# Contrast adjustment, streamed: from twelve tiles of 32 KB rows in six buffers to six tiles of 64 KB rows in three

## The chip, the cores and the metric

The kernel runs on one core of one Trainium2 chip. The core's engines appear in the profile under short names: PE is TensorE (its weight loads are PEld), DVE is VectorE, ACT is ScalarE, POOL is GpSimd and SP is SyncE. Data moves between the chip's main memory (DRAM) and the core's on-chip buffer (the SBUF, 128 partitions) by DMA, and sixteen DMA engines do the moving. A DMA is put into a queue by the engine that issues it: here SP issues all loads (the profile calls that queue q1) and ACT issues all stores (q10). The metric is the device time of one execution in microseconds (us), as the median of several runs. The hardware profiler recorded one execution; its lines are quoted with that execution's own times, counted from the start of its span.

## The reference

The input is sixteen images of three channels of 512 x 512 pixels in 32-bit floats, 50.33 MB. Every channel of every image is pulled away from its own mean and clipped:

```python
def reference(x, factor):                      # factor = 1.5
    mean = np.mean(x, axis=(2, 3), keepdims=True)
    return np.clip(mean + factor * (x - mean), 0, 1).astype(np.float32)
```

This is `clip(factor * x + (1 - factor) * mean)`. A channel's output cannot start before all of that channel has been read. Each byte has to be read once and written once: 100.66 MB in all.

## The kernel before

The input is seen as one flat run of numbers. A tile is 128 rows of ROW = 8192 numbers (32 KB), one row to a partition, 4.19 MB in all; a row is contiguous in DRAM. A channel has 262,144 pixels, so 32 neighbouring partitions hold one channel and a tile holds four channels. There are twelve tiles, t = 0 to 11. One SBUF tensor named ring holds six of them (BUFS = 6); tile t lies in place t modulo 6, and all work on it is done in place. With 32 KB per partition and tile, the ring takes 192 KB of each partition.

Four steps are done on a tile:

- `load(t)` (L82, on SP's queue) fetches the tile. The first two tiles come as one DMA each, tiles 2 and 3 as one DMA of 8.39 MB, tiles 4 and 5 as another, and the rest as one DMA each. From tile 6 on, a load may only begin when the store of the tile six before it has landed; SP waits for that before it issues the load.
- `add(t)` takes the sums. ACT copies the tile onto itself and accumulates a sum per partition (L96). For tile 0 alone the work is shared: DVE sums the first 4352 columns (L91) and ACT the other 3840. Then PE multiplies the sums by a matrix that adds up the 32 partitions of a channel and scales by (1 - factor) / 262144 (L100), and the result, called bias, stands in PSUM, one number per partition.
- `clip(t)` is two DVE instructions on the tile: times factor plus bias (L104), then the clip to 0 and 1 (L112).
- `store(t)` (L85, on ACT's queue) writes the tile out.

The order is written out by hand; each engine does its instructions in the order in which the program gives them, and waits where a result that it needs is not there. Tile 0 is clipped and stored in three pieces of 1024, 2048 and 5120 columns (FIRST gives the cuts), that is in rows of 4, 8 and 20 KB. After that comes a loop over the tiles: clip, then the sums of the next tile, then the store and a load:

```python
for t in range(1, n_tiles):
    clip(t)
    if t in (1, 3): store(t)
    if t + 1 < n_tiles: add(t + 1)
    if t not in (1, 3): store(t)
    if t + BUFS - 1 < n_tiles: load(t + BUFS - 1)
```

A store therefore stands on ACT mostly behind the sums of the next tile, and waits for the clip.

Of the kernel before, what the change touches and what calls it, by code (L numbers as in the profile page):

```python
# [1 line left out]

# [4 lines left out]


P = 128  # L10
ROW = 8192
BUFS = 6
FIRST = (1024, 3072)


@with_exitstack
def kernel(
    ctx: ExitStack,
    tc: tile.TileContext,
    x: bass.AP,  # L20
    factor: float,
    out: bass.AP,
):

    nc = tc.nc
    f32 = mybir.dt.float32
    Alu = mybir.AluOpType
    Act = mybir.ActivationFunctionType  # L30

    B, C, H, W = x.shape
    n_img, n_pix = B * C, H * W
    ppi = n_pix // ROW
    per_tile = P // ppi
    n_tiles = n_img // per_tile
    assert ppi * ROW == n_pix and per_tile * n_tiles == n_img

    factor = float(factor)
    wconst = (1.0 - factor) / float(n_pix)  # L40

    x_f = x.rearrange("b c h w -> (b c h w)")
    out_f = out.rearrange("b c h w -> (b c h w)")

    def dram(ap, t, c0=0, c1=ROW, n=1):
        run = [[P * ROW, n]] if n > 1 else []
        return bass.AP(
            tensor=ap.tensor, offset=t * P * ROW + c0, ap=[[ROW, P], *run, [1, c1 - c0]]
        )

    consts = ctx.enter_context(tc.tile_pool(name="consts", bufs=1))
    xpool = ctx.enter_context(tc.tile_pool(name="xpool", bufs=1))
    small = ctx.enter_context(tc.tile_pool(name="small", bufs=1))
    psum = ctx.enter_context(tc.tile_pool(name="psum", bufs=1, space=bass.MemoryType.PSUM))


    sums = small.tile([P, 2 * n_tiles], f32, name="sums")
    bias = psum.tile([P, n_tiles], f32, name="bias")

    blockw = consts.tile([P, P], f32, name="blockw")  # L60
    blocks = blockw.rearrange("p (a b) -> p a b", b=ppi)
    nc.gpsimd.memset(blockw, wconst)  # L62
    for base, step in ((0, -ppi), (ppi - 1, ppi)):
        nc.gpsimd.affine_select(  # L64
            out=blocks,
            in_=blocks,
            compare_op=Alu.is_ge,
            fill=0.0,
            base=base,
            pattern=[[step, per_tile], [0, ppi]],  # L70
            channel_multiplier=1 if step < 0 else -1,
        )


    ring = xpool.tile([P, BUFS, ROW], f32, name="ring")

    def slots(t, n=1, c0=0, c1=ROW):
        k = t % BUFS
        return ring[:, k, c0:c1] if n == 1 else ring[:, k : k + n, :]

    def load(t, n=1):
        nc.sync.dma_start(out=slots(t, n), in_=dram(x_f, t, n=n))  # L82

    def store(t, c0=0, c1=ROW):
        nc.scalar.dma_start(out=dram(out_f, t, c0, c1), in_=slots(t, 1, c0, c1))  # L85

    def add(t, c0=0):
        own = sums[:, 2 * t : 2 * t + 2]
        parts = []
        if c0:  # L90
            nc.vector.tensor_reduce(  # L91
                out=own[:, 0:1], in_=slots(t, 1, 0, c0), axis=mybir.AxisListType.X, op=Alu.add
            )
            parts.append(own[:, 0:1])
        part = slots(t, 1, c0)
        nc.scalar.activation(out=part, in_=part, func=Act.Copy, accum_out=own[:, 1:2])  # L96
        parts.insert(0, own[:, 1:2])
        shift = bias[:, t : t + 1]
        for k, part in enumerate(parts):
            nc.tensor.matmul(shift, blockw, part, start=k == 0, stop=k == len(parts) - 1)  # L100

    def clip(t, c0=0, c1=ROW):
        part = slots(t, 1, c0, c1)
        nc.vector.tensor_scalar(  # L104
            out=part,
            in0=part,
            scalar1=factor,
            scalar2=bias[:, t : t + 1],
            op0=Alu.mult,
            op1=Alu.add,  # L110
        )
        nc.vector.tensor_scalar(  # L112
            out=part, in0=part, scalar1=0.0, scalar2=1.0, op0=Alu.max, op1=Alu.min
        )

    with tc.manual_schedule():
        load(0)
        load(1)
        load(2, 2)
        load(4, 2)  # L120
        add(0, 4352)
        for c0, c1 in zip((0, *FIRST), (*FIRST, ROW)):
            clip(0, c0, c1)
            store(0, c0, c1)
        add(1)
        for t in range(1, n_tiles):
            clip(t)
            if t in (1, 3):
                store(t)
            if t + 1 < n_tiles:  # L130
                add(t + 1)
            if t not in (1, 3):
                store(t)
            if t + BUFS - 1 < n_tiles:
                load(t + BUFS - 1)


# [1 line left out]
_INS = ['x', 'factor']  # L139
_OUTS = [((16, 3, 512, 512), 'float32')]  # L140

_NUMBERS = {'factor': 1.5}


# [26 lines left out]
```

## Time and profile before

| | |
|---|---|
| median of 3 runs | 239.0 us (238.81 to 239.11) |
| the profiled execution | 238.72 us, of which the recorded span is 237.0 us |
| busy: DVE, ACT, PE | 112.1 us, 82.9 us, 7.6 us |
| bytes moved | 100.66 MB, 425 GB/s over the span |
| DMAs | 10 loads, 14 stores |
| time that the rows of the load queue and of the store queue took, as a share of the 16 DMA engines' span | 49.6% and 49.2% |

The page counts an engine as busy only while it computes. A DMA's issue is a short instruction on its engine's queue (SPq, ACTq), and its transfer runs on the DMA engines; the profile counts a DMA's rows as packets, and adds a small packet for each of the sixteen engines when a DMA ends. A view by windows gives, for chosen stretches of the span, how busy each engine was, how many instructions of it fell into the stretch (in brackets), the granted TensorE clock, the mean busy share of the DMA engines and the GB/s that they moved. In that view a row of a DMA counts in the stretch in which it starts, so a stretch that is not a whole number of rows long can show a little more or less than the true rate. The view of instructions in order of time has the start, the duration, the engine, the line, and in square brackets the idle time ahead of the instruction with what ended it.

### The profile page before, as it was taken

What the parts mean: (1) busy time and instruction counts of PE and PEld (TensorE: products, weight loads), DVE (VectorE), ACT (ScalarE), POOL (GpSimd) and SP (SyncE); (2) the same over time, 40 slices, a digit from 0 to 9 for tenths busy, and PEclk for the clock granted to TensorE, in tenths of its full rate; (3) what the DMA queues carried; (4) which work ended last, traced back from release to release, by engine and by line L of the source; (5) the groups of instructions that cost most, each with busy time, mean ns of one, the idle gap of its engine ahead of it and who ended that gap; (6) DMA issues with size and microseconds to landing.
All of it is one profiled execution on the core that took longest, in us unless ns stands there. A gap on an engine that the chain in (4) does not pass through costs nothing.

```text
span 237.0 us, 211 instructions
## 1 busy us (share of the span) xinstructions
PE 7.6 (3%) x26; PEld 6.5 (3%) x26; DVE 112.1 (47%) x29; ACT 82.9 (35%) x25; POOL 1.0 (0%) x7
## 2 busy tenths in 40 slices
PE   0000000000000000000000000000000000000000
PEld 0000000000000000000000000000000000000000
DVE  0078708609990059979209407704902920950000
ACT  2050190299100894650380091083056029000000
POOL 1000000000000000000000000000000000000000
DMA  7999998999999999999999999999999999999996
GB/s 265 442 442 442 398 459 383 441 428 435 465 426 404 409 442 442 442 442 442 442 426 431 404 420 442 442 442 442 442 442 426 415 398 442 442 442 442 442 442 265
DMA packets 3712, 100.66 MB, mean 425 GB/s; under 512 B 384, under 2 KB 384, under 8 KB 512
## 3 DMA queue, kind: packets, MB, share of 16 engines
q1 hardware_dynamic: 1696, 50.33, 49.6%
q10 hardware_dynamic: 2016, 50.33, 49.2%
HBM read 50.33 MB, written 50.33 MB: 425 GB/s over the span
## 4 chain that ended last, share of the span: by engine, by line
DMA 39%; DVE 25%; another core or an unknown queue 11%; ACT 9%; issue 3%; PE 1%; ACTq 1%; SPq 0%
DMA out_dram<-ring 20%; DMA ring<-in_x_dram 18%; DVE ring L104 11%; DVE ring L112 11%; ACT ring L96 9%; DVE sums L91 2%; PE bias L100 1%; ACTq L85 1%; SPq L82 0%
## 5 line engine op out<-in xcount | busy, mean ns | idle before, releaser
L96 ACT ACTIVATE ring<-ring 128x8192 f32<-128x8192 f32 (+1 forms) x12 | 80.7, 6724 | 117.3 <-DMA ring<-in_x_dram 95.3
L104 DVE TENSOR_SCALAR ring<-ring,bias 128x8192 f32<-128x8192 f32 (+3 forms) x14 | 54.3, 3880 | 84.9 <-PE bias L100 84.9
L112 DVE TENSOR_SCALAR ring<-ring 128x8192 f32<-128x8192 f32 (+3 forms) x14 | 53.4, 3817 | 0.5
L100 PE MATMUL bias<-sums,blockw 128*128 128x1 f32 x26 | 7.6, 361 | 194.0 <-ACT ring L96 193.5
L100 PEld LDWEIGHTS bias<-sums,blockw 128*128 128x128 f32 x26 | 6.5, 312 | 195.0 <-ACT ring L96 177.7
L91 DVE TENSOR_REDUCE sums<-ring 128x1 f32<-128x4352 f32 x1 | 4.7, 4685 | 13.1 <-DMA ring<-in_x_dram 13.1
L96 ACT ACTIVATION_READ_ACCUMULATOR ring<-ring 128x1 f32 x12 | 2.2, 186 | 0.0
L96 ACT ACT_TABLE_LOAD x1 | 1.3, 1283 | 0.8 <-PEq L152 0.8
L64 POOL TENSOR_SCALAR_AFFINE_SELECT blockw<-blockw 128x128 f32<-128x128 f32 x2 | 0.6, 311 | 0.1
L62 POOL MEMSET blockw<- 128x128 f32 x1 | 0.2, 204 | 0.3 <-POOLq L152 0.3
L152 POOL MEMSET const-uint8-127<- 128x1 uint8 x1 | 0.1, 103 | 0.0
L152 POOL MEMSET const-bfloat16-1.0<- 128x1 bf16 x1 | 0.1, 102 | 0.0
L152 POOL MEMSET const-float32-0.0<- 128x1 f32 x1 | 0.1, 98 | 0.3 <-issue 0.3
L152 POOL MEMSET const-float32-1.0<- 128x1 f32 x1 | 0.1, 98 | 0.0
## 6 DMA issues: line engine op xcount, KB each, us to landing
out_dram<-ring ACTq DMA_DIRECT2D x11, 4096.0 KB, 48.5
ring<-in_x_dram SPq DMA_DIRECT2D x8, 4096.0 KB, 31.4
ring<-in_x_dram SPq DMA_DIRECT2D x2, 8192.0 KB, 59.5
out_dram<-ring ACTq DMA_DIRECT2D x1, 2560.0 KB, 37.3
out_dram<-ring ACTq DMA_DIRECT2D x1, 1024.0 KB, 25.8
out_dram<-ring ACTq DMA_DIRECT2D x1, 512.0 KB, 16.1
```

The costliest lines, as they stand in the source:

```text
L62: nc.gpsimd.memset(blockw, wconst)
L64: nc.gpsimd.affine_select(out=blocks, in_=blocks, compare_op=Alu.is_ge, fill=0.0, base=base, pattern=[[step, per_tile], [0, ppi]], channel ...
L85: nc.scalar.dma_start(out=dram(out_f, t, c0, c1), in_=slots(t, 1, c0, c1))
L91: nc.vector.tensor_reduce(out=own[:, 0:1], in_=slots(t, 1, 0, c0), axis=mybir.AxisListType.X, op=Alu.add)
L96: nc.scalar.activation(out=part, in_=part, func=Act.Copy, accum_out=own[:, 1:2])
L100: nc.tensor.matmul(shift, blockw, part, start=k == 0, stop=k == len(parts) - 1)
L104: nc.vector.tensor_scalar(out=part, in0=part, scalar1=factor, scalar2=bias[:, t : t + 1], op0=Alu.mult, op1=Alu.add,)
L112: nc.vector.tensor_scalar(out=part, in0=part, scalar1=0.0, scalar2=1.0, op0=Alu.max, op1=Alu.min)
L152: nc = _bacc.Bacc("TRN2", target_bir_lowering=False, num_devices=1)
```

## The change

A tile becomes 128 rows of 16384 numbers (64 KB), 8.39 MB and eight channels. There are six tiles and three places in the ring, which still takes 192 KB of a partition. Sixteen neighbouring partitions hold a channel; the matrix for the sums is formed by the same code from the new number.

Loads and stores go by halves of the columns, 32 KB of each row and 4.19 MB in a DMA, except that the loads of the second and third tile (t = 1 and 2) and the store of the fifth (t = 4) are one DMA of whole 64 KB rows. A half takes every other 32 KB of the DRAM, as the rows are now 64 KB apart. Ten loads and eleven stores are issued. A load of tile t + 3 is issued half by half and waits for the landed store of what was in its place.

The sums of a tile are taken in three parts: ACT sums the first half, and 4608 columns of the second; DVE sums the last 3584. Three sums go through PE where there was one (two for tile 0). The clip works on halves, or on the whole tile where the store is whole. The three small first stores and the shared sum of tile 0 alone are gone. On ACT each store now stands ahead of the next tile's sums.

```diff
-ROW = 8192
-BUFS = 6
-FIRST = (1024, 3072)
+ROW = 16384
+HALF = ROW // 2
+BUFS = 3
+WHOLE = ((0, ROW),)
+HALVES = ((0, HALF), (HALF, ROW))
+SUM = 4608
...
+    def loads(t):
+        return WHOLE if t in (1, 2) else HALVES
+    def stores(t):
+        return WHOLE if t == 4 else HALVES
+    def load(t, k=0):
+        c0, c1 = loads(t)[k]
+        nc.sync.dma_start(out=cols(t, c0, c1), in_=dram(x_f, t, c0, c1))
+    def store(t, k=0):
+        c0, c1 = stores(t)[k]
+        nc.scalar.dma_start(out=dram(out_f, t, c0, c1), in_=cols(t, c0, c1))
+    def add(t):
+        own = sums[:, 3 * t : 3 * t + 3]
+        for k, (c0, c1) in enumerate(HALVES):
+            part = cols(t, c0, c1 - k * (HALF - SUM))
+            nc.scalar.activation(out=part, in_=part, func=Act.Copy, accum_out=own[:, k : k + 1])
+        nc.vector.tensor_reduce(
+            out=own[:, 2:3], in_=cols(t, HALF + SUM), axis=mybir.AxisListType.X, op=Alu.add
+        )
+        for k in range(3):
+            nc.tensor.matmul(
+                bias[:, t : t + 1], blockw, own[:, k : k + 1], start=k == 0, stop=k == 2
+            )
+    def clip(t, k=0):
+        part = cols(t, *stores(t)[k])
...
-        load(0)
-        load(1)
-        load(2, 2)
-        load(4, 2)
-        add(0, 4352)
-        for c0, c1 in zip((0, *FIRST), (*FIRST, ROW)):
-            clip(0, c0, c1)
-            store(0, c0, c1)
-        add(1)
-        for t in range(1, n_tiles):
-            clip(t)
-            if t in (1, 3):
-                store(t)
-            if t + 1 < n_tiles:
-                add(t + 1)
-            if t not in (1, 3):
-                store(t)
-            if t + BUFS - 1 < n_tiles:
-                load(t + BUFS - 1)
+        for t in range(BUFS):
+            for k in range(len(loads(t))):
+                load(t, k)
+        add(0)
+        for t in range(n_tiles):
+            for k in range(len(stores(t))):
+                clip(t, k)
+                store(t, k)
+                if t + BUFS < n_tiles:
+                    load(t + BUFS, k)
+            if t + 1 < n_tiles:
+                add(t + 1)
```

More of the change, by code (lines that the diff above doesn't have):

```diff
@@ L43, with dram @@
     out_f = out.rearrange("b c h w -> (b c h w)")
[L45 to L49, printed above, removed]
+    def dram(ap, t, c0=0, c1=ROW):
+        return bass.AP(tensor=ap.tensor, offset=t * P * ROW + c0, ap=[[ROW, P], [1, c1 - c0]])
     consts = ctx.enter_context(tc.tile_pool(name="consts", bufs=1))
@@ L54 @@
     psum = ctx.enter_context(tc.tile_pool(name="psum", bufs=1, space=bass.MemoryType.PSUM))
-    sums = small.tile([P, 2 * n_tiles], f32, name="sums")
+    sums = small.tile([P, 3 * n_tiles], f32, name="sums")
     bias = psum.tile([P, n_tiles], f32, name="bias")
@@ L75, with cols @@
     ring = xpool.tile([P, BUFS, ROW], f32, name="ring")
[L77 to L92, printed above, removed]
-            )
[L94 to L103, printed above, removed]
+    def cols(t, c0=0, c1=ROW):
+        return ring[:, t % BUFS, c0:c1]
+    def loads(t):
[19 more added lines that the diff above has]
+                bias[:, t : t + 1], blockw, own[:, k : k + 1], start=k == 0, stop=k == 2
+            )
+    def clip(t, k=0):
+        part = cols(t, *stores(t)[k])
         nc.vector.tensor_scalar(
```

## The prediction, made before the changed kernel was run

> **What bounds the kernel now.** I read the page's rows by engine first, then its DMA queues, the windows, the order of time, and last the chain.
>
> ```profile
> PE 7.6 (3%) x26; PEld 6.5 (3%) x26; DVE 112.1 (47%) x29; ACT 82.9 (35%) x25; POOL 1.0 (0%) x7
> q1 hardware_dynamic: 1696, 50.33, 49.6%
> q10 hardware_dynamic: 2016, 50.33, 49.2%
> ```
>
> No engine that computes is busy for half the span. The two DMA queues together hold the sixteen DMA engines for 98.8% of it. So the chain of waits (DMA 39%, DVE 25%, much of the rest unnamed) is a poor guide here: whichever instruction waits, the transfers run on. The windows show it:
>
> ```profile
> 0.00:1.80 1.80, 0.00 (x0) 0.00 (x0) 0.00 (x0) 1.00 (x1) 1.03 (x7) 1.00 0.00 0
> 1.80:12.13 10.33, 0.00 (x0) 0.00 (x0) 0.00 (x0) 0.28 (x1) 0.00 (x0) 1.00 1.02 412
> 20.00:76.40 56.40, 1.76 (x6) 1.50 (x6) 34.68 (x10) 21.26 (x6) 0.00 (x0) 1.00 1.00 428
> 31.49:54.50 23.01, 1.17 (x4) 1.00 (x4) 9.89 (x3) 12.96 (x5) 0.00 (x0) 1.00 1.01 425
> 99.00:176.45 77.45, 2.35 (x8) 2.01 (x8) 39.99 (x9) 28.49 (x9) 0.00 (x0) 1.00 1.00 433
> 195.80:234.50 38.70, 0.58 (x2) 0.50 (x2) 8.92 (x2) 5.19 (x2) 0.00 (x0) 1.00 1.00 434
> 234.60:237.00 2.40, 0.00 (x0) 0.00 (x0) 0.00 (x0) 0.00 (x0) 0.00 (x0) 1.00 0.04 14
> ```
>
> The last two numbers of a line are the DMA engines' share and GB/s. From 99 to 176 us loads and stores mix, from 195.8 on there are stores alone, and the rate is the same. The order of time gives it more exactly:
>
> ```profile
> 135.77 7.03 ACT L96 ACTIVATE ring<-ring 128x8192 f32<-128x8192 f32 x1 [12.23 <-DMA ring<-in_x_dram]
> ...
> 155.14 7.03 ACT L96 ACTIVATE ring<-ring 128x8192 f32<-128x8192 f32 x1 [12.25 <-DMA ring<-in_x_dram]
> ...
> 174.50 7.03 ACT L96 ACTIVATE ring<-ring 128x8192 f32<-128x8192 f32 x1 [12.23 <-DMA ring<-in_x_dram]
> ...
> 193.87 7.03 ACT L96 ACTIVATE ring<-ring 128x8192 f32<-128x8192 f32 x1 [12.25 <-DMA ring<-in_x_dram]
> ```
>
> ACT is released by a landed load every (193.87 - 135.77) / 3 = 19.37 us, and a load and a store of 4.19 MB each pass in that time: 9.68 us for 4.19 MB, 433.2 GB/s. All 100.66 MB at this rate take 24 x 9.68 = 232.4 us. The other 4.6 us of the span are: 1.8 before the first byte; 10.33 - 9.68 = 0.65 on the first load; about 1.2 at the end (rows stop starting by 234.6, and a row holds its engine for 9.68 / 8 = 1.2, so data flows until 235.8); and the remaining 1.0 us between 12 and 76 us, where the 428 and 425 stand. That is the stretch of the small first stores, and the only one in which rows of unequal size share the engines. 49.6% against 49.2% for the same bytes says that it is the load queue's rows that took longer.
>
> **What the change can reach.** The 232.4 us stay: the bytes are the same. The 1.8, the 0.65 and the 1.2 stay too: the first load is again a 4.19 MB DMA from an idle queue, and the last store a 4.19 MB DMA by 32 KB rows. Two questions are left: what becomes of the 1.0 us, and whether the DMA queues ever both run empty.
>
> *Small rows.* The 384 rows of 4, 8 and 20 KB go. If their 1.0 us goes with them and nothing comes instead, the span is 236.0. But a new unequal mix comes: 64 KB loads beside 32 KB stores, from the first store (about 37 us) to the end of the third load (about 71 us), some 34 us. The bounds: no loss, as in the equal mix (433); or the loss of the worst window, (433 - 425) / 433 = 1.9% of 34 us = 0.6 us. The nearest row is the whole mixed stretch, 428 with 20 KB rows in most of it: 1.2% of 34 us is 0.4. Rows that are larger than before rather than smaller should lose less, so I take 0.2.
>
> *Fewer rows.* Three whole tiles save 24 rows on each engine. A cost per row, as such, hardly shows: the store queue's 1792 data rows (2016 packets less 14 x 16 at the ends of DMAs) took no longer than the load queue's 1536. At most it is the 1.0 us spread over the 16 rows that the three pieces of tile 0 add on each engine, 0.06 us each, 1.5 us for 24; at least nothing. I take 0.1 us of gain, near the lower end, for that row.
>
> *Compute.* ACT sums 8192 columns in 7.03 us and 3840 in 3.40, so 4608 take 4.05 and 0.19 to read out; DVE sums 4352 columns in 4.69, so 3584 take 3.86; PE takes 0.6 for one sum (two instructions), 0.9 for three at most; a clip of 8192 columns is 4.49 + 4.43. From the last half landed to the first store: 4.25 + 0.9 + 8.95 = 14.1 us, and a tile with its data there costs 7.2 + 4.25 + 0.9 + 17.9 = 30.3 us, against 2 x 19.37 = 38.7 us of transfers. DVE rises by 6 x 3.9 - 4.7 = 19 us to about 131 and ACT falls to 6 x (7.2 + 4.25) + 1.3 = 70. All of it is covered while a queue has work. The stores that now stand ahead of the next sums on ACT hold those sums up until both clips are done; that is in the 30.3, and its price is in the following schedule.
>
> *The queues.* I take it that two queues with work alternate row by row: equal rows share evenly (the 19.37 above), and the 512 KB store at 20.0 us, which took 16.1 us to land, needed about the 128 rows of 32 KB that alternated with its 128 (4.7 MB, 10.9 us) and not twice its bytes (2.4 us). Then, in us, with 64 KB against 32 KB the load gets two thirds:
> - First tile: halves land at 13.1 and 22.8; its stores issue at 22.8 + 14.1 = 36.9 and 45.9. Loads alone keep the engines busy until then: by 36.9 they moved 34.5 x 433 = 14.9 of 25.2 MB. The rest needs 10.2 / 289 = 35 us beside store 0a, which lands near 68 (4.19 / 144 = 29 us).
> - Compute then sets the stores: 1a 67, 1b 76, 2a 98, 2b 107, 3a 128, 3b 137. Each finds the queue full: store landings come at 68, 86, 105, 125, 144, 163, 183, 196.
> - Loads wait for those landings: 3a issues at 69 (the load queue ends at 71), 3b at 87, 4a 106, 4b 126, 5a 145, 5b 164; each is issued some 5 us ahead of the end of the one before it, except 3b and 4a, where a short pause leaves the engines to the stores. Loads 4b and 5b land near 151 and 190.
> - The whole store 4 issues at 151 + 5.1 + 17.9 = 174, behind 3b, and lands near 215. Store 5a issues at 190 + 14.1 = 204, 11 us before store 4 is through; 5b at 213, while 5a runs to 225. 5b ends at 235.
>
> So I find no time at which both queues are empty; the least cover is the 11 us at the last tile.
>
> **Sum.** 237.0 - 1.0 + 0.2 - 0.1 = 236.1 us of span. Outside the span lie 238.72 - 237.0 = 1.72 us, giving 237.8; the profiled execution stands 0.28 below the median of the runs, so the median comes to 238.1 us, 0.4% below 239.0.
>
> **The rivals.**
>
> *No difference.* The new mix loses what the old one lost, its 0.6 us and another half on the way in and out of the mix (store 4's large rows beside load 5b are a second, short one). For it: what slowed the rows is not named by any view, and unequal size is the only feature that I could match to the place. Against: bigger rows. Then the 1.0 us is back: 239.0.
>
> *A hole before the last tile, slower.* If load 5b lands more than 11 us later than my 190, the engines stand still between the end of store 4 and the start of 5a, and each further us is a us on the end. For it: only three places in the ring, every load behind a landed store, and the 5 us between a load's issue and the end of the one ahead, which is little where the lag from issue to first byte is unknown under load (1.0 us at the start, idle). If 64 KB loads got only an even share at the start, while store 4 kept its double one, the same schedule puts 5b at 203 and a hole of up to 3 us: 241. Against: the 11 us.
>
> *Slower transfers, slower.* The distance between the rows in DRAM doubles from 32 to 64 KB, and half DMAs skip every other 32 KB. If this lowers the rate, each percent is 2.3 us; with 0.65% (1.5 us) the kernel is slower than before by more than 0.2%. At 2%, the loss of the worst window, the time is 238.1 + 4.6 = 243. Against: the rate did not care about the direction or the mix of equal rows. The Trainium skill has a rule that speaks for it (DMA: Bandwidth & Descriptors, Latency and other measured facts): large power-of-two distances between partitions' rows in DRAM cost rate, 207 GB/s at 512 KiB against 214 padded. An estimate by that page's 3.3% would add 7.6 us and give 246, but its table does not reach down to 64 KB, and no run so far shows such a distance.
>
> *Not as described.* If 64 KB rows are cut into 32 KB ones on their way, all shares are even; my schedule then has load 5b near 197 to 200 and still no hole: 238.2, within the forecast.
>
> **How the numbers follow.** Forecast (with the last rival) 0.62, its own range 237.6 to 238.5; no difference 0.18; hole 0.10; slower transfers 0.10. About 0.2%, 0.5 us, is what a measurement of this kernel can tell from no change: 238.5 to 239.5. That gives faster 0.62, same 0.18, slower 0.20. The range runs from 237.4, where the mix costs nothing and rows save 0.5, to 241.0, where the hole has its price; above lies the half of the slower transfers, and some of the bigger holes.
>
> **What would show it.** Right: windows after 75 us at 433 GB/s, the mixed stretch 37 to 71 us above 428, both queues near 49.2 to 49.4%, store 5a issued near 204 us, no window before 234 well under 425. A hole would show as a window with less than 0.9 of the DMA engines near 215 us. Slower transfers would show as stores alone at the end below 433, or as landings more than 19.37 us apart. My schedule is wrong if load 5b lands far from 190 us.

## The result, and the profile after

The changed kernel takes 239.8 us (median of 11 runs, 239.49 to 241.75) against 238.97 us before; the ratio is 1.0057, with a 95% interval of 1.0031 to 1.0083. It is slower by about half a percent where 0.4% faster was predicted, though the time lies inside the stated range (237.4 to 241.0). The eleven times fall into two groups: seven from 239.49 to 239.82 us and four from 241.0 to 241.75. The profiled execution (241.0 us, span 239.3) is one of the upper group. In the experiments below, one run of e2 (243.94 us), one of f1 (244.6) and five of f2 (254 to 257) are over 1.5% above the fastest run of their kernel and stay out of the figures.

The page of the changed kernel, its engines and its two DMA queues:

```profile
PE 9.6 (4%) x36; PEld 8.6 (4%) x36; DVE 129.3 (54%) x28; ACT 68.6 (29%) x25; POOL 1.1 (0%) x7
q1 hardware_dynamic: 1440, 50.33, 49.4%
q10 hardware_dynamic: 1584, 50.33, 48.8%
```

Compute is as forecast (DVE about 131, ACT about 70), still far from the span, and the queues hold the DMA engines for 98.2% of it. The windows of the same execution; the last two numbers of a line are the DMA engines' share and GB/s:

```profile
12.13:36.30 24.17, 1.57 (x6) 1.43 (x6) 12.17 (x3) 11.26 (x4) 0.00 (x0) 1.00 1.01 438
38.60:43.60 5.00, 0.00 (x0) 0.00 (x0) 4.97 (x2) 0.00 (x0) 0.00 (x0) 1.00 1.03 341
46.00:70.00 24.00, 1.60 (x6) 1.43 (x6) 14.96 (x4) 11.15 (x4) 0.00 (x0) 1.00 1.01 437
99.00:176.45 77.45, 3.20 (x12) 2.86 (x12) 48.59 (x10) 22.52 (x8) 0.00 (x0) 1.00 1.00 433
235.50:236.50 1.00, 0.00 (x0) 0.00 (x0) 0.00 (x0) 0.00 (x0) 0.00 (x0) 1.00 0.23 98
236.50:237.50 1.00, 0.00 (x0) 0.00 (x0) 0.00 (x0) 0.00 (x0) 0.00 (x0) 1.00 0.15 66
```

The kernel before has, in two windows of its mixed stretch and in those at its own end:

```profile
33.00:38.00 5.00, 0.59 (x2) 0.50 (x2) 1.64 (x1) 2.69 (x2) 0.00 (x0) 1.00 0.91 381
47.00:52.00 5.00, 0.00 (x0) 0.00 (x0) 0.00 (x0) 5.00 (x1) 0.00 (x0) 1.00 1.08 446
234.50:235.50 1.00, 0.00 (x0) 0.00 (x0) 0.00 (x0) 0.00 (x0) 0.00 (x0) 1.00 0.23 98
235.50:236.50 1.00, 0.00 (x0) 0.00 (x0) 0.00 (x0) 0.00 (x0) 0.00 (x0) 1.00 0.01 0
```

Three things are to be seen. The rate of equal rows is the old one, 433 GB/s, with rows 64 KB apart. The stretch in which 64 KB load rows alternate with 32 KB store rows (46 to 70 us) loses nothing. The loss is in two other places.

One is five microseconds around 40 us at 341 GB/s with the DMA engines fully busy: single rows took longer there. The rate alone does not say so, since in a window this short it depends on how many rows happen to start in it; the share beside it does. The rows that start in this window take 1.03 x 5 = 5.15 us of each engine, and at 433 GB/s their bytes would take 341 x 5 / 433 = 3.94: 1.2 us lost. The same sum gives 0.15 and 0.25 us for the two windows of the kernel before. I call such a loss a dip.

The other place is the end. Between 235.5 and 236.5 us three rows of 32 KB start (98 KB), in the next microsecond two (66 KB), while the other engines are done; the kernel before ends with one such microsecond fewer. I call that engines out of step. The small packets with which the sixteen engines end the last store stand 2.0 us apart in the changed kernel and 0.35 us in the kernel before.

The order of time gives the places to set against the predicted schedule:

```profile
12.97 7.03 ACT L98 ACTIVATE ring<-ring 128x8192 f32<-128x8192 f32 x1 [10.89 <-DMA ring<-in_x_dram]
...
36.97 9.26 ACTq L92 DMA_DIRECT2D out_dram<-ring  x2
...
194.75 4.04 ACT L98 ACTIVATE ring<-ring 128x4608 f32<-128x4608 f32 x1 [8.33 <-DMA ring<-in_x_dram]
...
209.04 9.24 ACTq L92 DMA_DIRECT2D out_dram<-ring  x2
```

The first line is also a ruler. When the first load has landed, 23 more units of 4.19 MB have to pass, 23 x 9.68 = 222.6 us; what the span has beyond that grows with whatever is lost. It is no full account of the loss, because a landing is reported when the engines are already at the next unit; it compares kernels, to some 0.3 us (by it e9 below lies 0.3 us above e3, while their last rows end within 0.1 us of each other). The kernel before lands its first load at 13.11 and needs 237.0 - 13.11 = 223.9 us from there. The changed kernel needs 239.3 - 12.97 = 226.3, 2.4 us more. The ruler leaves out the start, so it is used for the runs below.

### The profile page after: what moved, and what is told of

Same layout as the page of the kernel before. It is cut to its first block, busy times and chain, and to the rows that moved or that the text cites. A ratio compares the mean times of both kernels' runs of the same rounds, so it can differ in the third digit from the quotient of the medians.

```text
span 239.3 us, 224 instructions
## 1 busy us (share of the span) xinstructions
PE 9.6 (4%) x36; PEld 8.6 (4%) x36; DVE 129.3 (54%) x28; ACT 68.6 (29%) x25; POOL 1.1 (0%) x7
## 3 DMA queue, kind: packets, MB, share of 16 engines
q1 hardware_dynamic: 1440, 50.33, 49.4%
## 4 chain that ended last, share of the span: by engine, by line
DMA 41%; DVE 26%; ACT 13%; another core or an unknown queue 8%; PE 2%; issue 0%; SPq 0%; ACTq 0%; DVEq 0%
DMA ring<-in_x_dram 21%; DMA out_dram<-ring 20%; DVE ring L109 13%; DVE ring L117 13%; ACT ring L98 13%; PE bias L103 2%; SPq L88 0%; ACTq L92 0%; DVEq L109 0%
## 5 line engine op out<-in xcount | busy, mean ns | idle before, releaser
L98 ACT ACTIVATE ring<-ring 128x8192 f32<-128x8192 f32 (+1 forms) x12 | 66.4, 5533 | 129.5 <-DVE ring L117 97.0
L109 DVE TENSOR_SCALAR ring<-ring,bias 128x8192 f32<-128x8192 f32 (+1 forms) x11 | 53.6, 4876 | 23.7 <-PE bias L103 23.7
L99 DVE TENSOR_REDUCE sums<-ring 128x1 f32<-128x3584 f32 x6 | 23.3, 3883 | 64.5 <-DMA ring<-in_x_dram 64.5
L117 DVE TENSOR_SCALAR ring<-ring 128x8192 f32<-128x8192 f32 (+1 forms) x11 | 53.0, 4815 | 0.4
L103 PE MATMUL bias<-sums,blockw 128*128 128x1 f32 x36 | 9.6, 358 | 190.4 <-ACT ring L98 190.4
L103 PEld LDWEIGHTS bias<-sums,blockw 128*128 128x128 f32 x36 | 8.6, 319 | 191.3 <-ACT ring L98 171.1
```

Of the source, the lines that this page charges most:

```text
L99: nc.vector.tensor_reduce(out=own[:, 2:3], in_=cols(t, HALF + SUM), axis=mybir.AxisListType.X, op=Alu.add)
L103: nc.tensor.matmul(bias[:, t : t + 1], blockw, own[:, k : k + 1], start=k == 0, stop=k == 2)
L109: nc.vector.tensor_scalar(out=part, in0=part, scalar1=factor, scalar2=bias[:, t : t + 1], op0=Alu.mult, op1=Alu.add,)
L117: nc.vector.tensor_scalar(out=part, in0=part, scalar1=0.0, scalar2=1.0, op0=Alu.max, op1=Alu.min)
```

## The experiments

Theory A at the start: 64 KB load rows, in flight when the first store begins, cost the time. The rivals: the first store costs it whatever the load's rows (B), or the large rows of store 4 do (C).

**e1: loads 1 and 2 by halves, store 4 whole**

```diff
-        return WHOLE if t in (1, 2) else HALVES   # loads
+        return HALVES
```

> Loads 1 and 2 by halves (32 KB rows); store 4 stays whole. The profile of the changed kernel shows 341 GB/s from 38.6 to 43.6 us, where the first 32 KB store rows meet 64 KB load rows in flight. Theory A (64 KB load rows at the first store cost about 1.2 us, and what they leave behind costs more: engines out of step to the end): this loss goes, no window before 70 us falls under 420 GB/s, and the time is 238.0 to 238.6 us, unless the schedule's hole opens (store 4 through before store 5a is issued, up to 3 us more, seen as a window near 216 us with under 0.9 of the DMA engines). Theory B (the loss comes with the first store whatever the load's rows, or with the halves that skip every other 32 KB): the dip near 39 us stays, the time stays at 239.5 to 241.8 us.

**e2: store 4 by halves, loads 1 and 2 whole**

```diff
-        return WHOLE if t == 4 else HALVES        # stores
+        return HALVES
```

> Only store 4 goes by halves; loads 1 and 2 stay whole. Theory A: the dip near 39 us stays, the time stays at 239.5 to 241.8 us. Theory C (the large rows of store 4 near the end, beside load 5b and ahead of store 5a, leave the engines out of step and cost the 1 to 2 us): the time falls to about 238.3 us.

**e3: everything by halves** (both edits)

> All loads and stores by halves, every row 32 KB. Theory A: as equal rows only, 433 GB/s from 12 us on but for the first meeting of loads and stores, 237.9 to 238.4 us, and the schedule has no hole here (store 4b behind 4a, load 5b near 200 us). Theory B: 239.5 us or more, since nothing but the row size of three tiles has changed.

Measured: e1 239.84 us (239.47 to 241.11), e2 239.69 (239.51 to 241.58), e3 239.53 (239.30 to 239.77, ratio to the kernel before 1.0025, interval 1.0016 to 1.0034). Windows of e3, where all rows are 32 KB:

```profile
38.60:43.60 5.00, 0.00 (x0) 0.00 (x0) 4.96 (x2) 0.00 (x0) 0.00 (x0) 1.00 1.05 354
99.00:176.45 77.45, 3.19 (x12) 2.85 (x12) 43.97 (x11) 22.52 (x8) 0.00 (x0) 1.00 1.00 433
```

The dip is there with equal rows as well, and by the sum of share and rate it loses the same 1.2 us: theory A is wrong as to the dip, and B is right. The trace's record of single rows places it. In e3 the slow rows are the last one or two load rows of each engine ahead of the first row of the first store, which starts at 42.3 us, 5.4 us after its issue: these load rows take up to 2.2 us in place of 1.21, and the store's own rows none longer. What has gone in e3 is the upper group and part of the loss: 237.6 - 12.89 = 224.7 us on the ruler, against 226.3. e2 keeps both groups, so C is wrong. e1 has another reason, which the prediction had as a rival. These are a window of e1, whose profile is of a run of 240.68 us, and the issue of its stores 5a and 5b:

```profile
215.00:219.00 4.00, 0.00 (x0) 0.00 (x0) 4.00 (x2) 0.00 (x0) 0.00 (x0) 1.00 0.31 131
...
217.21 9.24 ACTq L92 DMA_DIRECT2D out_dram<-ring  x2
```

Store 4 with its double share is through before store 5a has been issued at 217.2 us (209.0 in the changed kernel), and the DMA engines stand idle: from 216 to 218 us no row starts at all.

**e4: the kernel before with tile 0 clipped and stored as a whole**

```diff
-FIRST = (1024, 3072)
+FIRST = ()
```

> The kernel before with tile 0 clipped and stored as a whole, so that all its rows are 32 KB too. The prediction's term: the 1.0 us between 12 and 76 us goes with the small rows, 238.0 us. Rival: the 1.0 us belongs to the first meeting of loads and stores, or to something else in that stretch, and stays: 239.0 us.

Measured: 242.54 us (242.50 to 243.05), ratio 1.0156 (1.0142 to 1.0169). Without its small first rows the kernel before is not 1.0 us faster but 3.6 us slower, outside both expectations. The ruler gives 240.9 - 12.98 = 227.9. Windows of e4:

```profile
28.50:33.50 5.00, 0.00 (x0) 0.00 (x0) 0.00 (x0) 5.00 (x1) 0.00 (x0) 1.00 0.89 315
99.00:176.45 77.45, 2.34 (x8) 2.00 (x8) 43.87 (x10) 33.18 (x9) 0.00 (x0) 1.00 1.00 429
237.50:238.50 1.00, 0.00 (x0) 0.00 (x0) 0.00 (x0) 0.00 (x0) 0.00 (x0) 1.00 0.23 98
```

The dip comes just after this kernel's first store, issued at 27.5 us; then the mixture of equal rows does not reach 433, and at the end the engines are out of step (three rows still start after 237.5 us). So the dip goes with the first meeting of loads and stores. But it is not the whole price: here the dip loses 0.89 x 5 - 315 x 5 / 433 = 0.8 us, less than in e3, and most of the 3.6 us comes after it, in the slower mixture and in engines that drift apart (the packets that end a load stand 0.9 us apart at 52 us and 4.8 at 205). The small first rows were not a cost but a remedy.

The next four ask what the dip hangs on. Theory F: one row of the first store per engine. Theory G: the first write to DRAM is slow.

**e5: all halves, and a tiny early store**

```diff
+    warm = consts.tile([P, 128], f32, name="warm")
+    nc.gpsimd.memset(warm, 0.0)
     with tc.manual_schedule():
+        nc.scalar.dma_start(out=dram(out_f, 5, 0, 128), in_=warm)
```

> All halves, as the third experiment (239.5 us), and before anything else a store of 128 rows of 512 bytes of zeros to columns of the output's last tile, which that tile's own store overwrites some 200 us later. The third experiment lost about 1.1 us per DMA engine in load rows between 38 and 42 us, just ahead of the first store's first rows (354 GB/s from 38.6 to 43.6). Theory G (the first write to DRAM is slow, whenever it comes): the loss goes with the early store, no dip near 39 us, about 238.4 us. Theory F (the loss is one row of the first store per engine, so it grows with that row): unchanged, 239.5 us, with the dip near 39 us.

**e6: all halves, the first half of tile 0 stored in three pieces once it is clipped**

```diff
                 clip(t, k)
-                store(t, k)
+                if t == 0 and k == 0:
+                    for c0, c1 in ((0, 1024), (1024, 3072), (3072, HALF)):
+                        nc.scalar.dma_start(out=dram(out_f, 0, c0, c1), in_=cols(0, c0, c1))
+                else:
+                    store(t, k)
```

> All halves, but the first half of tile 0, once it is clipped as a whole, goes out in three stores of 1024, 2048 and 5120 columns, as the kernel before did. Theory F: the first rows are 4 KB, the loss at the first meeting falls from 1.1 us to a few tenths, 238.4 to 238.9 us. Theory G: unchanged at 239.5 us, with the dip near 39 us.

**e7: the kernel before, its three pieces stored only after the whole clip**

```diff
+        clip(0)
         for c0, c1 in zip((0, *FIRST), (*FIRST, ROW)):
-            clip(0, c0, c1)
             store(0, c0, c1)
```

> The kernel before, with tile 0 clipped as a whole and only then stored in its three pieces: the time of the first store is that of the fourth experiment (27.5 us, 242.5 us in all), its row sizes are those of the kernel before (239.0 us). Theory F (row size): 238.9 to 239.4 us. Rival (the time at which the first store starts, or the shape of the clips): 242.5 us.

**e8: all halves, but the store of tile 0 as one DMA of 64 KB rows**

```diff
-        return HALVES                              # stores
+        return WHOLE if t == 0 else HALVES
...
-                    load(t + BUFS, k)
+                    for j in (0, 1) if t == 0 else (k,):
+                        load(t + BUFS, j)
```

> All halves, but the store of tile 0 is one DMA of 64 KB rows; both half loads of tile 3 wait for it. Theory F: the loss at the first meeting (now near 47 us) grows to about two rows of 32 KB, 2.4 us, 240.7 us or more with engines further out of step. Theory G: it stays near 1.1 us, 239.5 us.

Measured: e5 239.88 us (239.72 to 240.07), e6 239.28 (239.08 to 240.01, ratio 1.0016, 1.0007 to 1.0026), e7 239.39 (238.68 to 241.04, ratio 1.0020, 1.0000 to 1.0040), e8 239.43 (239.37 to 239.78). The window of e5 around the first large store:

```profile
38.60:43.60 5.00, 0.00 (x0) 0.00 (x0) 4.97 (x2) 0.00 (x0) 0.00 (x0) 1.00 0.99 315
```

and that of e8 around its own, which comes later:

```profile
46.60:51.60 5.00, 0.00 (x0) 0.00 (x0) 2.61 (x1) 5.00 (x1) 0.00 (x0) 1.00 1.21 419
```

G is out: a store at the very start leaves the dip as it was (1.3 us by the sum). F is half right. Small first rows shrink the loss: e7 starts its first store as late as e4 and wins back 3.1 of the 3.6 us, with two late times of 240.4 and 241.0 left; e6 gains 0.25 us on e3. In recorded spans e6 gains all of it: the median of its runs is 237.3 us, as that of the kernel before, against 237.8 in e3. What e6 still takes longer lies outside the span (2.0 us against 1.7), where no view reaches. But 64 KB first rows (e8) cost no more than 32 KB ones (239.43 against 239.53, and the dip is again 1.2 us), so the loss is not one row of the store long.

The next ones look at the two groups. **e9 is the changed kernel again**, for a second profile.

> The changed kernel itself, unaltered, for a second profile: its eleven times fell into two groups, 239.5 to 239.8 and 241.0 to 241.8 us, and the profile is of the upper one. There the engines finish the last store 2.0 us apart (0.35 us in the kernel before). Theory A (the loss of the upper group is engines out of step since the first meeting of loads and stores): a profile of the lower group has its last landings under 1.5 us apart and the same dip near 39 us. Rival: the same spread in both, and the difference lies elsewhere, such as a slower first load.

**e10 and e11: stores by halves, and of the loads only load 1, or only load 2, whole**

```diff
-        return WHOLE if t in (1, 2) else HALVES   # loads
+        return WHOLE if t == 1 else HALVES        # e10
+        return WHOLE if t == 2 else HALVES        # e11
```

> Of the 64 KB rows only load 1 is left; load 2 and all stores go by halves. Load 1's last rows are the ones in flight when the first store begins (38.6 us). If 64 KB rows in flight at that moment throw the engines out of step: times in two groups as with both loads whole, 239.5 to 241.8 us, median over 239.7. If it is the following mixture of 64 KB loads with 32 KB stores: as with all halves, 239.3 to 239.8 us, in one group.

> Of the 64 KB rows only load 2 is left. In flight at the first meeting are 32 KB rows of load 1; the mixture of 64 KB load rows with 32 KB store rows follows from about 42 to 60 us. If the rows in flight at the meeting matter: 239.3 to 239.8 us, one group. If the mixture matters: two groups, 239.5 to 241.8 us.

Measured: e9 six times from 239.51 to 239.65 us and two at 241.6, its profile in the lower group (239.58, span 237.8, 225.0 on the ruler); e10 239.58 in one group (239.44 to 239.77); e11 240.13 in two (239.37 to 239.55, and 240.72 to 242.34). The end of e9, and then the end of e11, whose profile is of its upper group:

```profile
38.60:43.60 5.00, 0.00 (x0) 0.00 (x0) 4.96 (x2) 0.00 (x0) 0.00 (x0) 1.00 0.97 315
235.50:236.50 1.00, 0.00 (x0) 0.00 (x0) 0.00 (x0) 0.00 (x0) 0.00 (x0) 1.00 0.01 0
```

```profile
235.50:236.50 1.00, 0.00 (x0) 0.00 (x0) 0.00 (x0) 0.00 (x0) 0.00 (x0) 1.00 0.08 33
236.50:237.50 1.00, 0.00 (x0) 0.00 (x0) 0.00 (x0) 0.00 (x0) 0.00 (x0) 1.00 0.08 33
237.50:238.50 1.00, 0.00 (x0) 0.00 (x0) 0.00 (x0) 0.00 (x0) 0.00 (x0) 1.00 0.08 33
```

The same kernel in its lower group has the same dip, but its engines finish together. In e11 one row of 32 KB (33 KB, a share of 0.08) starts in each of three microseconds: the kernel waits for one engine. So the difference between the groups is engines out of step. How far apart the sixteen engines end a DMA shows when that comes about (us between the first and the last of their small packets):

| kernel | load that ends at 42 to 45 us | store that ends at 60 to 72 us | last store |
|---|---|---|---|
| before | 0.39 | 0.30 | 0.35 |
| e9, changed, lower group | 0.47 | 0.47 | 0.47 |
| changed, upper group | 2.29 | 2.89 | 2.04 |
| e11, load 2 whole, upper group | 0.93 | 4.05 | 3.39 |
| e10, load 1 whole | 2.03 | 2.17 | 1.02 |
| e3, all halves | 1.91 | 1.40 | 0.49 |

The dip can throw the engines apart by itself, but e3 and e10 come back together by the end and have one group of times. In e11 they part between the end of load 1 (43 us) and that of the first half-store (69 us). The upper group comes with the 64 KB rows of load 2, which run beside the first stores, not with those of load 1, which are in flight at the first meeting.

**e12: all halves, the first half of tile 0 clipped and stored in three pieces, early**

```diff
+    def clip(t, k=0, cut=None):
+        part = cols(t, *(cut or stores(t)[k]))
...
+                if t == 0 and k == 0:
+                    for c0, c1 in ((0, 1024), (1024, 3072), (3072, HALF)):
+                        clip(0, cut=(c0, c1))
+                        nc.scalar.dma_start(out=dram(out_f, 0, c0, c1), in_=cols(0, c0, c1))
...
```

> All halves, and the first half of tile 0 clipped and stored in three pieces of 1024, 2048 and 5120 columns, each store issued as soon as its piece is clipped, as the kernel before does. If nothing but the first meeting separates the new tiling from the kernel before, this equals the kernel before: 238.8 to 239.1 us. If halves of 64 KB rows cost something by themselves: 239.3 us or more, as with the pieces stored late (239.28).

Measured: 241.0 us (240.84 to 241.29), worse than with the same pieces stored late. Its windows have new dips:

```profile
75.00:80.00 5.00, 0.00 (x0) 0.00 (x0) 5.00 (x2) 2.48 (x1) 0.00 (x0) 1.00 1.03 413
85.00:90.00 5.00, 1.29 (x6) 1.12 (x5) 0.16 (x1) 3.66 (x2) 0.00 (x0) 1.00 0.96 360
```

That is where the load queue, empty since load 2, starts again. In the changed kernel, too, the third load ends near 72 us, close to the landing of the first store on which the next load waits. Hence a new theory: a load queue that starts again from empty, with engines out of step, makes the upper group.

**f1: the changed kernel, the first half-store and the load that waits for it each in two DMAs of every other partition**

```diff
                 clip(t, k)
+                if t == 0 and k == 0:
+                    for p in (0, 1):
+                        rows = lambda ap, u: bass.AP(
+                            tensor=ap.tensor,
+                            offset=(u * P + p) * ROW,
+                            ap=[[2 * ROW, P // 2], [1, HALF]],
+                        )
+                        there = ring[p:P:2, 0, 0:HALF]
+                        nc.scalar.dma_start(out=rows(out_f, 0), in_=there)
+                        nc.sync.dma_start(out=there, in_=rows(x_f, 3))
+                    continue
                 store(t, k)
```

> The changed kernel, with the store of tile 0's first half and the load of tile 3's first half each as two DMAs of every other partition (32 KB rows as before, four to a DMA engine in place of eight). The first half-store lands near 57 us, so the next load is in its queue well before the third load ends near 72 us: the load queue no longer runs empty, and all 64 KB rows stay. Theory A (an empty load queue that starts again while the engines are out of step makes the upper group): one group of times, 239.4 to 239.9 us. Theory B (the mixture of 64 KB and 32 KB rows makes it by itself): two groups, as before, 239.5 to 241.8 us.

**f2: e12, with load 3a in the same three pieces**

```diff
                         nc.scalar.dma_start(out=dram(out_f, 0, c0, c1), in_=cols(0, c0, c1))
+                        nc.sync.dma_start(out=cols(3, c0, c1), in_=dram(x_f, 3, c0, c1))
+                    continue
```

> The twelfth experiment (all halves, early small pieces of tile 0, 240.8 to 241.3 us), whose load queue was empty from about 71 to 76 us because load 3a waited for all three pieces; here load 3a goes in the same three pieces, each behind its own store, so the queue stays filled. Theory A: the slow rows near 75 and 85 us go and the time falls to 238.9 to 239.3 us. Theory B (small rows that start early are themselves the loss in this tiling): 240.8 us or more.

Measured: f1 241.29 us (240.02 to 243.0), more scattered than the changed kernel. A window of it, and then one of f2 (247.88 us in its profiled run) with the issue of its last stores:

```profile
70.00:75.00 5.00, 0.00 (x0) 0.00 (x0) 4.96 (x2) 0.00 (x0) 0.00 (x0) 1.00 0.99 367
```

```profile
218.00:224.00 6.00, 0.00 (x0) 0.00 (x0) 5.97 (x3) 0.00 (x0) 0.00 (x0) 1.00 0.01 5
...
224.00 9.24 ACTq L92 DMA_DIRECT2D out_dram<-ring  x2
```

In f1 a second dip stands at 70 to 75 us, where the load queue goes from 64 KB to 32 KB rows, and the scatter stays, though the load queue no longer runs empty near 70 us: an empty queue is not needed for it. Nor is it enough, since in e9, of the lower group, no load row starts between 69.5 and 73.9 us. f2 says nothing on it: from 72 to 90 us, while its loads go by 4 and 8 KB rows, the load queue moves 1.3 MB and the store queue 6.5 (3.4 and 4.2 in the changed kernel). The last tile comes late, and six microseconds stand empty ahead of store 5a, issued at 224 us. It is the hole of the prediction's second rival, and a larger one.

**g1 and g2: the kernel before with two first pieces, and with four**

```diff
-FIRST = (1024, 3072)
+FIRST = (2048,)             # g1
+FIRST = (512, 1536, 3584)   # g2
```

> The kernel before with tile 0 in two pieces, of 2048 and 6144 columns (8 and 24 KB rows), in place of three from 4 KB. If small first rows are the remedy for the first meeting and a coarser start is a worse one: between the kernel before (239.0) and one piece (242.5), 239.3 to 241.5 us. If small rows cost by themselves, as predicted: 238.7 us, fewer small rows than before.

> The kernel before with tile 0 in four pieces, of 512, 1024, 2048 and 4608 columns (2, 4, 8 and 18 KB rows). If a gentler start helps further: 238.6 to 238.9 us, below both kernels. If three pieces had already got what there is: 239.0 us. If small rows cost by themselves: 239.3 us or more.

Measured: g1 239.25 us (239.08 to 239.69, ratio 1.0014, 1.0005 to 1.0023), g2 239.93 (239.0 to 240.15, ratio 1.0039, 1.0026 to 1.0053). One piece costs 3.6 us and two 0.3; three are the kernel before; four are worse again, by 1.0 (five runs, 239.0 to 240.15). Small first rows help, but not the more the smaller. No version that was run has a median below the kernel before.

The ruler, from the first landed load to the end of the span, in the profiles that carry the reading (222.6 us are the 23 units alone):

| kernel | span | first load landed | from there to the end |
|---|---|---|---|
| before | 237.0 | 13.11 | 223.9 |
| e7, late small pieces | 237.1 | 13.02 | 224.1 |
| e3, all halves | 237.6 | 12.89 | 224.7 |
| e9, changed, lower group | 237.8 | 12.83 | 225.0 |
| changed, upper group | 239.3 | 12.97 | 226.3 |
| e11, load 2 whole, upper group | 240.6 | 12.83 | 227.8 |
| e4, before with one first store | 240.9 | 12.98 | 227.9 |

## Why the prediction was wrong, step by step

*What bounds the kernel* was right: transfers at 433 GB/s in both kernels. Compute was hidden in all of the runs but e1 and f2, where the DMA engines stood idle for the last tile's sums and clips.

*The ledger of the 4.6 us* had a term that was too large. It put 1.0 us, what the other terms had left over, into the stretch from 12 to 76 us. One window of the kernel before covers that stretch:

```profile
12.13:77.60 65.47, 2.90 (x10) 2.50 (x10) 40.85 (x13) 24.75 (x8) 0.00 (x0) 1.00 1.01 431
```

At 431 GB/s it is 0.3 us short of 433; by the record of single rows, its rows took 0.6 us of each engine more than such rows take in the steady stretch. The sign that was read from the queues, 49.6% against 49.2%, is about 0.95 us, but the 0.65 us of the first load, already counted, is part of it. So no more than some 0.6 of the 1.0 us was there to be won.

*Small rows* is the step that failed, the term of -1.0 us. The prediction put the loss down to rows of unequal size and let it go with the small stores. e4 did just that and lost 3.6 us; e7 put small rows back at nearly the same time of issue and lost 0.4. In the new tiling, e3, without small rows, is 0.6 us above the kernel before, and e6, with them, is level with it in the span. What the small rows hold down begins at the first meeting of loads and stores: every kernel with a first store of 32 KB rows or more shows a dip there, of 0.8 us in e4 and 1.2 to 1.3 in the changed kernel, e3, e5, e8 and e9, whether its loads have 32 KB rows or 64 KB rows. In the kernel before the loss is smaller and spread out (0.15 and 0.25 us in two windows 14 us apart). The change took the remedy away with the supposed cost.

*The new mixture*, taken at 0.2 us with 0.6 as its bound, was sized by the wrong kind of loss: a rate times the length of the mixture. The mixture itself runs at 437 GB/s from 46 to 70 us and costs nothing by its rate. In the lower group it costs nothing that these runs can tell (six times of e9 lie between 239.51 and 239.65 us, the median of e3 is 239.53). Its price is the upper group, some 2 us in four of eleven runs, by engines out of step. That the time lies inside the range all the same is luck: the range reached up to 241.0 for a hole that did not open. The rival "no difference" came nearest, but it too had the loss as a rate and not above the old one.

*Fewer rows*, 0.1 us of gain, is not to be seen: e3, which has more rows, is no slower than the lower group.

*The queues.* The shares and the schedule were right in kind: first store issued 36.97 (predicted 36.9), load 5b landed 194.75 (190), store 5a issued 209.0 (204), no hole. Of the signs of being right, "no window before 234 well under 425" fails around 40 us; but it was no sharp sign, as the kernel before has a window at 381 GB/s (33 to 38 us). The hole was a real neighbour: e1 fell into it with a double share for store 4 and none for the loads, the condition that the rival named. *Not as described* falls: the page counts 1440 packets in the load queue, which are 1024 rows of 32 KB, 256 of 64 KB and 160 ends of DMAs, so the rows kept their size; and store 5a was issued at 209.0 us, with 32 KB load rows (e1) at 217.2.

*Slower transfers* falls too. With rows 64 KB apart the changed kernel, e3 and e9 move 433 GB/s from 99 to 176 us. The Trainium skill's rule on large power-of-two row distances (DMA: Bandwidth & Descriptors, Latency and other measured facts) shows no effect at this distance; its figures begin at 512 KiB, which no run here tried.

What stays open is what happens in the dip. It isn't the first write (e5), doesn't grow with store rows from 32 to 64 KB (e8), and is weaker with smaller ones (e6, e7). Why e4 goes on losing after its dip, and the changed kernel hardly does, is open too. Nor is it known why the 64 KB rows of load 2 leave one or a few engines behind in some executions and not in others; only that they do (e10 against e11), that an empty load queue isn't needed for it (f1), and that the kernel then waits for the last engine.

## What to carry to other kernels

In a kernel like this one, which fills its DMA queues all the time, the bytes and the rate set nearly everything, and what is left is in transitions: the first load, the first meeting of loads and stores, the end. A loss that stands beside an odd-looking feature in the profile may be what that feature is holding down; a version without the feature, run alone, tells which. Give the first store small rows at first, but try how many, and look at the last microseconds by windows: a few rows a microsecond there mean that the kernel waits for a few engines that fell out of step. Read the rate of a short window only together with its DMA share.

## What had not been expected of the hardware

When the first large store joined a running stream of loads, the sixteen DMA engines lost about a microsecond each way it was tried (0.8 us in e4, 1.2 to 1.3 in five others), while counting as busy. The rows that took longer were the last load rows ahead of the store's first row: in e9 sixteen load rows of 64 KB that start near 39 us take 3.5 to 3.8 us in place of 2.42, and the first store row starts after them, at 42.5 us. Once engines are out of step they can stay so for the rest of the kernel: in e11 they ended the first half-store (69 us) 4.05 us apart and the last 3.39, with one engine at work for the last three microseconds. And the loss is sensitive to how the store begins: in the kernel before, one first piece took 242.5 us, two 239.25, three 239.0 and four 239.9.
